# A differential-attention norm: its small VectorE operations moved behind the query's evacuation and cut from fifteen to eleven

## The chip, the cores and the metric

One core of a Trainium2 chip runs the whole kernel as one launch. The metric is device time in microseconds (us), the median of repeated runs. The engines are TensorE (PE for matmuls, PEld for weight loads), VectorE (DVE), ScalarE (ACT), GpSimd (POOL) and SyncE (SP), which issues most DMAs. Each engine works through its own queue strictly in order, so an instruction that waits holds back everything queued behind it on that engine.

## The reference, cut to what matters

Two layers run one after the other on 512 tokens of width 1024: sparse attention, then differential attention. Only the second is touched here:

```python
# differential attention: 8 heads, two softmax maps each, 128 value columns per head
p = softmax(where(dist >= 0, q @ k.T / 8 + bias, NEG))      # [heads, 2 maps, 512, 512]
a = p[:, 0] - lam * p[:, 1]
o = a @ v                                                   # per head: [512, 128]
o = rmsnorm(o, subln) * (1 - lambda_init)                   # over the 128 columns of a head
o = o.reshape(512, 1024) * silu(z)
return o @ w_out                                            # then x + rmsnorm(...)
# rmsnorm(o) = o / sqrt(mean(o * o) + 1e-6) * g
```

The kernel leaves the softmax undivided and divides later. With den0 and den1 the sums of the two maps' exponentials, it forms `p1 * lam * den0 / den1 - p0`, which is den0 times the wanted difference, up to the sign.

## The kernel before, in words

The differential layer goes through eight heads, and in a head through four blocks of 128 queries (units) in the order 3, 0, 2, 1. A unit covers 512, 128, 384 and 256 keys respectively. For each of its two maps, a unit has two score matmuls into an S bank of PSUM (lines 806 and 807; two S banks alternate between the maps), one DVE instruction that adds the bias and takes the row minimum (line 798), and one ACT exponential with its sum (line 800). After the second map DVE takes the reciprocal (1147), a factor (1148) and the difference (1149, in SBUF). TensorE then transposes the difference (1157), ACT copies it out (1159), and TensorE multiplies it with the values (1167). ACT copies a head's result o out of PSUM (1171).

Between these, a runner inserts the input projections of later heads: one job (`mjob`) is 24 matmuls of 512 columns (line 197). When a job is over, POOL splits the next raw weights into a high and a low part (lines 164 and 166, four pieces each), and the job's PSUM result is evacuated. For a query job that is `evac_q`: for each of two map halves ACT writes the rounded part (line 99) and then DVE the remainder (line 428), both by turns on the same bank. A unit's first score matmul (line 806) of the next head needs this remainder.

The norm is done once for a pair of heads. `dhead1` has eight ACT squares with sums (1179), then the small DVE operations on tiles of 128 by 8: two products with the reciprocal of den0 (1183), the mean and epsilon (320), an inverse square root from an integer start value by two correction steps (322 to 334), and a last product (1186). Then come eight products of o with the factor and the gate (1190, 128x128 each, both operands in SBUF). `dhead2` transposes o on TensorE (1198) and splits it again on ACT and DVE (99, 1201) as an operand of the output projection.

`dhead1` of heads 0 and 1 is issued in head 2 after the second unit, that of heads 2 and 3 in head 4, that of 4 and 5 in head 6, and that of 6 and 7 after the last head. The program is written in this order with priorities, and a scheduler sets the order of each engine's queue when the kernel is built. `issue_after(ins)` keeps the instructions of a block behind `ins` on its engine.

Of the kernel before, what the change touches and what calls it, by code (L numbers as in the profile page):

```python
# [57 lines left out]
EPS = 1e-6  # L58
# [9 lines left out]
def trunk(ctx: ExitStack, tc: tile.TileContext, x, table, npre, npost, w_in, pe_k, w1_k, w2_k,  # L68
# [248 lines left out]
    def rsqrt(y, ss, n, scale):  # L317

        m = small(n, tag="rs1")
        nc.vector.tensor_scalar(m, ss, scale, EPS, op0=OP.mult, op1=OP.add)  # L320
# [4 lines left out]
        w = small(n, tag="rs4")  # L325
        nc.vector.tensor_tensor(q, y, y, op=OP.mult)
        nc.vector.tensor_tensor(q, q, m, op=OP.mult)
        nc.vector.tensor_scalar(q, q, -0.5, 1.5, op0=OP.mult, op1=OP.add)
        nc.vector.tensor_tensor(y, y, q, op=OP.mult)
        nc.vector.tensor_tensor(q, y, y, op=OP.mult)  # L330
        nc.vector.tensor_tensor(q, q, m, op=OP.mult)
        nc.vector.tensor_scalar(w, q, 0.375, -1.25, op0=OP.mult, op1=OP.add)
        nc.vector.tensor_tensor(w, w, q, op=OP.mult)
        nc.vector.scalar_tensor_tensor(y, w, 1.875, y, op0=OP.add, op1=OP.mult)
# [87 lines left out]
    def evac_q(get, h0):  # L422
        def f(p):
            for j in range(2):
                t = get(h0 + j)
                a = slice(64 * j, 64 * j + 64)
                hi(t[0:64], p[a], 0.125)
                nc.vector.scalar_tensor_tensor(t[64:128], p[a], 0.125, t[0:64].bitcast(F32),
                                               op0=OP.mult, op1=OP.subtract)
# [283 lines left out]
    def turn_small():  # L713
# [7 lines left out]
        nc.scalar.activation(subT, pp[:, 0:8], AF.Copy, scale=-0.5 * (1.0 - LAMBDA_INIT))  # L721
# [402 lines left out]
    class DUnit:  # L1124
# [8 lines left out]
        def a(self, m):  # L1133
# [7 lines left out]
            self.P.append(softmap(s, n, 2 * h + m, qb, st[:, m:m + 1], st[:, 4 + m:5 + m]))  # L1141
            if m:
                p0, p1 = self.P
                if h % 2 == 0 and self.first:
                    T["rr", h // 2] = small(16, tag="drr", bufs=2)
                rr = T["rr", h // 2].rearrange("p (m c) -> p c m", m=2)[:, h % 2 * 4 + qb]
                nc.vector.reciprocal(rr, st[:, 4:6])
                nc.vector.tensor_scalar(st[:, 8:9], rr[:, 1:2], lam, st[:, 4:5], op0=OP.mult, op1=OP.mult)
# [25 lines left out]
    def dhead1(h0):  # L1174
# [6 lines left out]
        rr = T["rr", h0 // 2][:, 0:8]  # L1181
        for _ in range(2):
            nc.vector.tensor_tensor(ss, ss, rr, op=OP.mult)
        r = small(8, tag="drs")
        rsqrt(r, ss, 8, 1.0 / 128)
        nc.vector.tensor_tensor(r, r, rr, op=OP.mult)
# [93 lines left out]
```

## Time and profile before

| | |
|---|---|
| time, median of 3 runs | 656.49 us (655.78 to 656.52) |
| profiled execution, its own time | 655.29 us |
| span of its trace | 653.3 us |
| mean granted TensorE clock | 0.995 of full speed |
| TensorE busy | 635.7 us, 97% of the span |
| VectorE, ScalarE, GpSimd busy | 406.2, 344.7 and 401.4 us |

The differential heads run from about 424 to 601 us of the span, and the output projection fills the rest. A row of a timeline gives the start and duration of an instruction, its engine and line, what it writes and reads, and in brackets the idle time before it with what ended it.

### The profile page before, as it was taken

To read this page: it belongs to the slowest core of one execution; us is meant where nothing else is said; L and a number is where in the kernel's file an instruction comes from. 1 tells how busy PE (TensorE), PEld (TensorE's weight loads), DVE (VectorE), ACT (ScalarE), POOL (GpSimd) and SP (SyncE) were. 2 spreads that over 40 slices of the span, in tenths; PEclk is the share of its full clock that TensorE was granted. 3 is DMA by queue.
4 is the path that set the end of the run, shared out by engine and by line. 5 is a ranking of instruction groups with operands and counts; after the bars stand their busy time and mean duration, and the time that the engine had idled before them with its cause. 6 is when DMAs were issued, how large, how long until landed. Compare 5 with 4: busy or idle time off the path is not lost.

```text
span 653.3 us, 11250 instructions
## 1 busy us (share of the span) xinstructions
PE 635.7 (97%) x3767; PEld 554.5 (85%) x3767; DVE 406.2 (62%) x1190; ACT 344.7 (53%) x914; POOL 401.4 (61%) x675
## 2 busy tenths in 40 slices
PE   8999999999999999999999999999999998989996
PEld 6988888888888788788888899898987987879885
DVE  5512335678878878869788700235568669797634
ACT  6321234677667667768565411335474575668431
POOL 5458668778677687768585658848664554522300
PEclk9999999999999999999999999999999999989998
DMA  7636433213022121201962132423233232215302
GB/s 250 175 88 159 129 81 89 57 34 72 26 65 67 33 64 30 53 17 37 290 198 98 65 97 68 127 65 114 65 82 81 73 79 61 66 64 199 125 28 101
DMA packets 68847, 60.00 MB, mean 92 GB/s; under 512 B 3613, under 2 KB 60853, under 8 KB 68790
## 3 DMA queue, kind: packets, MB, share of 16 engines
q1 hardware_dynamic: 68068, 56.93, 29.7%
q10 hardware_dynamic: 722, 2.36, 0.9%
q8 instruction: 30, 0.49, 0.3%
q14 instruction: 27, 0.22, 0.1%
HBM read 54.52 MB, written 4.76 MB: 91 GB/s over the span
## 4 chain that ended last, share of the span: by engine, by line
PE 85%; DVE 8%; ACT 3%; issue 2%; DMA 1%; SPq 0%; DVEq 0%; ACTq 0%
PE mm L197 31%; PE mm L220 12%; PE mm L474 6%; PE S L220 6%; PE av L876 6%; PE T L862 5%; PE S L807 4%; PE S L806 4%; PE S L474 3%; PE av L1167 2%; PE T L727 1%; PE T L1157 1%; DMA wraw<-in_nsa_w_in_dram 1%; DVE stk L104 1%; DVE P L798 1%
## 5 line engine op out<-in xcount | busy, mean ns | idle before, releaser
L166 POOL TENSOR_TENSOR wlo<-wraw,whi 128x256 fp32r<-128x256 f32 (+2 forms) x247 | 182.7, 767 | 23.7 <-ACT whi L162 23.1
L164 POOL TENSOR_SCALAR whi<-wraw 128x256 fp32r<-128x256 f32 (+1 forms) x240 | 96.5, 428 | 101.4 <-PE mm L197 58.5
L800 ACT ACTIVATE P<-P,st 128x512 f32<-128x512 f32 (+3 forms) x192 | 107.4, 560 | 83.9 <-DVE st L798 83.1
L856 POOL TENSOR_SCALAR P<-P,st,gate 128x512 f32<-128x512 f32 (+3 forms) x128 | 80.2, 638 | 25.7 <-DVE st L853 17.6
L798 DVE CUSTOM_DVE_ANT_0 P<-S,BT 128x128 f32<-128x128 f32 (+2 forms) x144 | 59.7, 418 | 28.5 <-PE S L807 26.2
L197 PE MATMUL mm<-bigA,whi 128*128 128x512 f32 x192 | 77.1, 402 | 0.1
L197 PE MATMUL mm<-bigA,wlo 128*128 128x512 f32 x192 | 75.5, 393 | 0.0
L197 PE MATMUL mm<-bigB,whi 128*128 128x512 f32 x192 | 75.3, 392 | 0.0
L104 DVE TENSOR_TENSOR PT<-T,PT 128x512 fp32r<-128x512 f32 x84 | 56.9, 685 | 7.3 <-ACT PT L99 5.0
L876 PE MATMUL av<-PT,bigE 128*128 128x512 f32 x160 | 57.3, 418 | 0.1
L104 DVE TENSOR_TENSOR stk<-mm,stk 64x512 fp32r<-64x512 f32 x32 | 22.0, 689 | 52.2 <-ACT stk L99 51.8
L99 ACT ACTIVATE PT<-T 128x512 fp32r<-128x512 f32 x84 | 48.3, 593 | 8.8 <-PE T L862 6.1
L862 PE MATMUL T<-ident,P 128*128 128x128 f32 x320 | 52.1, 272 | 0.0
L197 PE MATMUL mm<-bigF,whi 128*128 128x512 f32 x128 | 51.4, 402 | 0.0
L99 ACT ACTIVATE stk<-mm 64x512 fp32r<-64x512 f32 x64 | 37.9, 592 | 25.1 <-PE mm L197 13.9
L862 PEld LDWEIGHTS T<-ident,P 128*128 128x128 f32 x320 | 40.8, 140 | 11.8 <-DVE PT L104 0.2
L220 PE MATMUL mm<-whi,bigF 128*128 128x256 f32 x176 | 50.7, 289 | 0.1
L197 PE MATMUL mm<-bigE,whi 128*128 128x512 f32 x128 | 50.4, 394 | 0.0
L220 PE MATMUL mm<-wlo,bigF 128*128 128x256 f32 x176 | 50.3, 286 | 0.0
L197 PE MATMUL mm<-bigF,wlo 128*128 128x512 f32 x128 | 50.2, 392 | 0.0
L220 PE MATMUL mm<-whi,bigE 128*128 128x256 f32 x176 | 49.8, 284 | 0.0
L197 PEld LDWEIGHTS mm<-bigB,whi 128*128 128x128 f32 x192 | 36.1, 188 | 8.0
(295 smaller groups left out, 1646.4 us busy)
## 6 DMA issues: line engine op xcount, KB each, us to landing
wraw<-in_diff_w_in_dram SPq DMA_DIRECT2D x31, 512.0 KB, 3.9
wraw<-in_nsa_w_in_dram SPq DMA_DIRECT2D x26, 512.0 KB, 3.8
BT<-rd SPq DMA_DIRECT2D x32, 128.0 KB, 3.2
wraw<-in_diff_w_out_dram SPq DMA_DIRECT2D x5, 512.0 KB, 3.8
wraw<-in_nsa_w_out_dram SPq DMA_DIRECT2D x4, 512.0 KB, 3.5
bigD<-in_x_dram SPq DMA_DIRECT2D x4, 512.0 KB, 3.8
x1d<-bigD ACTq DMA_DIRECT2D x4, 512.0 KB, 2.6
bigF<-x1d SPq DMA_DIRECT2D x4, 512.0 KB, 6.2
```

The lines of the kernel that those rows point to most:

```text
L99: return nc.scalar.activation(dst, src, AF.Copy, scale=scale)
L104: nc.vector.tensor_tensor(dst, src, h.bitcast(F32), op=OP.subtract)
L164: nc.gpsimd.tensor_scalar(h[:, a:b], v, 1.0, 0.0, op0=OP.mult, op1=OP.add)
L166: e.tensor_tensor(l[:, a:b], v, h[:, a:b].bitcast(F32), op=OP.subtract)
L197: T["mm"] = nc.tensor.matmul(p[:, a:b], wt[:, k, :], u[:, k, a:b], start=(k == 0 and j == 0), stop=(k == KD - 1 and j == 2)).ins
L220: nc.tensor.matmul(acc[t], u[:, k0 + k, t * 128:(t + 1) * 128], wt[:, k, :], start=(ci == 0 and k == 0 and j == 0 and t % per == 0), stop= ...
L474: nc.tensor.matmul(p, U[u][:, k, t * 128:(t + 1) * 128], wt[wi], start=start and j == 0, stop=stop and j == 2, skip_group_check=True)
L798: nc.vector.tensor_tensor_reduce(out=o, in0=i0, in1=b, op0=OP.add, op1=OP.min, scale=-1.0, scalar=BIG, accum_out=nm)
L800: nc.scalar.activation(pt[:, :n], pt[:, :n], AF.Exp, bias=nm, scale=-1.0, accum_out=den)
L856: NORM(nc, i, br, qb).tensor_scalar(self.P[i][:, :n], self.P[i][:, :n], st[:, 8 + i:9 + i], gate[:, NT - 1 - qb, c:c + 1], op0=OP.mult, op ...
L862: T["tmark"] = nc.tensor.transpose(p[:, j * 128:(j + 1) * 128], self.P[j][:, kb * 128:(kb + 1) * 128], ident).ins
L876: nc.tensor.matmul(av, T["V"][:, br, kb, g, :], p, start=(br == 0 and kb == 0 and j == 0), stop=(br == 1 and kb == qb and j == 1))
```

## The change

The norm's formula is multiplied through by den0. In place of o/den0 · 1/sqrt(mean(o²)/den0² + eps) the kernel computes o · 1/sqrt(mean(o²) + eps·den0²): two operations form `den0 * den0 * eps + ss / 128`, and the products with the reciprocal go. The correction steps are written with fewer instructions; a constant factor 0.375 of the second one is moved into `subT`. The fifteen small DVE operations of a norm become eleven, nine of which have two tensors in SBUF as operands. The sum den0 is written by the exponential straight into a tile that lives for a pair of heads, and the reciprocal in a unit takes one column in place of two.

`dhead1` keeps only the eight ACT squares and stays where it was. The rest is now `dnorm`, called after a head's last projection job, under `issue_after(T["qe"])`, where `T["qe"]` is the last remainder of a query evacuation (line 428 before, 426 now). `dhead2` for the same heads moves from the third and fourth units of heads 2, 4 and 6 to the second and third units of heads 3, 5 and 7.

```diff
-    def rsqrt(y, ss, n, scale):
+    def rsqrt(y, ss, d, n, scale):
         m = small(n, tag="rs1")
-        nc.vector.tensor_scalar(m, ss, scale, EPS, op0=OP.mult, op1=OP.add)
+        nc.vector.scalar_tensor_tensor(m, d, EPS, d, op0=OP.mult, op1=OP.mult)
+        nc.vector.scalar_tensor_tensor(m, ss, scale, m, op0=OP.mult, op1=OP.add)
         sh = small(n, I32, tag="rs2")
...
-        nc.vector.tensor_tensor(q, y, y, op=OP.mult)
-        nc.vector.tensor_tensor(q, q, m, op=OP.mult)
-        nc.vector.tensor_scalar(q, q, -0.5, 1.5, op0=OP.mult, op1=OP.add)
-        nc.vector.tensor_tensor(y, y, q, op=OP.mult)
-        nc.vector.tensor_tensor(q, y, y, op=OP.mult)
-        nc.vector.tensor_tensor(q, q, m, op=OP.mult)
-        nc.vector.tensor_scalar(w, q, 0.375, -1.25, op0=OP.mult, op1=OP.add)
-        nc.vector.tensor_tensor(w, w, q, op=OP.mult)
-        nc.vector.scalar_tensor_tensor(y, w, 1.875, y, op0=OP.add, op1=OP.mult)
+        nc.vector.tensor_tensor(q, y, m, op=OP.mult)
+        nc.vector.scalar_tensor_tensor(q, q, -0.5, y, op0=OP.mult, op1=OP.mult)
+        nc.vector.scalar_tensor_tensor(y, q, 1.5, y, op0=OP.add, op1=OP.mult)
+        nc.vector.tensor_tensor(q, y, m, op=OP.mult)
+        nc.vector.tensor_tensor(q, q, y, op=OP.mult)
+        nc.vector.scalar_tensor_tensor(q, q, -10.0 / 3, q, op0=OP.add, op1=OP.mult)
+        nc.vector.scalar_tensor_tensor(y, q, 5.0, y, op0=OP.add, op1=OP.mult)
@@ class DUnit, a(m)
-                nc.vector.reciprocal(rr, st[:, 4:6])
-                nc.vector.tensor_scalar(st[:, 8:9], rr[:, 1:2], lam, st[:, 4:5], op0=OP.mult, op1=OP.mult)
+                nc.vector.reciprocal(st[:, 6:7], st[:, 5:6])
+                nc.vector.tensor_scalar(st[:, 8:9], st[:, 6:7], lam, den, op0=OP.mult, op1=OP.mult)
@@ def dhead1(h0), after the eight squares
-        rr = T["rr", h0 // 2][:, 0:8]
-        for _ in range(2):
-            nc.vector.tensor_tensor(ss, ss, rr, op=OP.mult)
+        T["dss"] = ss
+
+    def dnorm(h0):
+        ss = T["dss"]
         r = small(8, tag="drs")
-        rsqrt(r, ss, 8, 1.0 / 128)
-        nc.vector.tensor_tensor(r, r, rr, op=OP.mult)
+        rsqrt(r, ss, T["den", h0 // 2], 8, 1.0 / 128)
         for i in range(8):
...
-            if i in (2, 3) and h in (2, 4, 6):
+            if i in (1, 2) and h in (3, 5, 7):
                 dhead2(h - 4 + i)
             carry = u
         run.upto(dends[h])
+        if h in (2, 4, 6):
+            with tc.issue_after(T["qe"]):
+                dnorm(h - 2)
     carry.t(0)
     carry.v(0)
     dhead1(6)
+    dnorm(6)
     dhead2(6)
```

Line numbers of the rows after the norm's own are two lower in the changed file (798 is 796, 1190 is 1188). Up to the second unit of head 2 every engine's queue holds the same work in the same order, and POOL and SP do so throughout.

First place, DVE's queue at the end of head 2. Names: `rs`, `drs` and `dss` are the norm's small tiles, `drr` the sums or reciprocals, `stk` a query or key operand, `PT` a head's o, `P` the softmax tiles, `st` a unit's columns. Before:

```order
L332 TENSOR_SCALAR rs_5936<-rs_5935 128x8
L798 ISA P,st<-S,BT_80 128x256
L798 ISA st 128x1
L333 TENSOR_TENSOR rs_5936<-rs_5936,rs_5935 128x8
L428 SCALAR_TENSOR_TENSOR stk<-mm,stk 64x512
L334 SCALAR_TENSOR_TENSOR drs<-rs_5936,drs 128x8
L1147 RECIPROCAL drr<-st 128x2
L1186 TENSOR_TENSOR drs<-drs,drr 128x8
L1148 TENSOR_SCALAR st<-drr,lam,st 128x1
L1190 SCALAR_TENSOR_TENSOR PT<-PT,drs,bigB 128x128 x8
L1149 SCALAR_TENSOR_TENSOR P<-P,st 128x256
L428 SCALAR_TENSOR_TENSOR stk<-mm,stk 64x512
```

The same place on DVE in the changed kernel:

```order
L796 ISA P,st<-S,BT_80 128x256
L796 ISA st 128x1
L426 SCALAR_TENSOR_TENSOR stk<-mm,stk 64x512
L1145 RECIPROCAL st<-st 128x1
L1146 TENSOR_SCALAR st<-st,lam,drr 128x1
L1147 SCALAR_TENSOR_TENSOR P<-P,st 128x256
L426 SCALAR_TENSOR_TENSOR stk<-mm,stk 64x512
L320 SCALAR_TENSOR_TENSOR rs_6023<-drr 128x8
L321 SCALAR_TENSOR_TENSOR rs_6023<-dss,rs_6023 128x8
L323 TENSOR_SCALAR rs_6026<-rs_6023 128x8
L324 TENSOR_SCALAR drs<-rs_6026 128x8
L796 ISA P,st<-S,BT_80 128x512
```

All of the norm has moved behind both remainders; the other seven small operations and the eight products follow the last row shown, ahead of the second 128x512 row of line 796.

Second place, DVE's queue at the start of head 5, from the remainder on. Before, where the norm of heads 2 and 3 is already over:

```order
L428 SCALAR_TENSOR_TENSOR stk<-mm,stk 64x512
L798 ISA P,st<-S,BT_79 128x512
L798 ISA st 128x1
L1201 SCALAR_TENSOR_TENSOR bigD<-T,subT,bigC 128x512 x2
L798 ISA P,st<-S,BT_79 128x512
L798 ISA st 128x1
L798 ISA P,st<-S,BT_79 128x128
```

And now, from the seventh of the eleven operations on:

```order
L329 TENSOR_TENSOR drs<-drs,rs_6581 128x8
L796 ISA P,st<-S,BT_79 128x512
L796 ISA st 128x1
L330 TENSOR_TENSOR rs_6587<-rs_6587,drs 128x8
L331 SCALAR_TENSOR_TENSOR rs_6587<-rs_6587 128x8
L332 SCALAR_TENSOR_TENSOR drs<-rs_6587,drs 128x8
L1188 SCALAR_TENSOR_TENSOR PT<-PT,drs,bigB 128x128 x8
L1145 RECIPROCAL st<-st 128x1
L796 ISA P,st<-S,BT_79 128x128
```

The eight products now stand ahead of the 128x128 bias rows that free the S banks of the second unit.

## Rows read from the trace of the kernel before

**Rows 1.** Page, busy us (share of the span) x instructions of each engine
```profile
PE 635.7 (97%) x3767; PEld 554.5 (85%) x3767; DVE 406.2 (62%) x1190; ACT 344.7 (53%) x914; POOL 401.4 (61%) x675
```

**Rows 2.** Waits of PE, 410 to 605 us: total us, times, longest us
```profile
PE S L806 <- DVE stk L428: 4.7, 4, 1.9
```

**Rows 3.** Windows: us, busy of PE PEld DVE ACT POOL, PEclk, DMA share, GB/s
```profile
540.00:550.00 10.00, 8.07 (x46) 6.43 (x46) 9.74 (x32) 4.90 (x11) 4.27 (x8) 1.00 0.23 69
...
580.00:590.00 10.00, 8.29 (x54) 7.91 (x55) 8.21 (x32) 4.47 (x13) 0.00 (x1) 0.83 0.16 52
```

**Rows 4.** Timeline of PE, ends of heads 4 and 6: start, duration, instruction
```profile
544.44 0.50 PE L806 MATMUL S<-stk 128*128 128x512 f32 x1 [1.93 <-DVE stk L428]
...
581.71 0.79 PE L806 MATMUL S<-stk 128*128 128x512 f32 x1 [1.90 <-DVE stk L428]
...
582.73 0.41 PE L220 MATMUL mm<-whi,bigF 128*128 128x256 f32 x1
582.94 0.41 PE L220 MATMUL mm<-wlo,bigF 128*128 128x256 f32 x1
...
584.86 0.40 PE L220 MATMUL mm<-whi,bigF 128*128 128x256 f32 x1
...
585.82 0.28 PE L220 MATMUL mm<-wlo,bigF 128*128 128x256 f32 x1
585.94 0.28 PE L220 MATMUL mm<-whi,bigE 128*128 128x256 f32 x1
```

**Rows 5.** Timeline of DVE, end of head 2
```profile
494.79 0.69 DVE L332 TENSOR_SCALAR rs<-rs 128x8 f32<-128x8 f32 x1
...
496.20 0.69 DVE L428 SCALAR_TENSOR_TENSOR stk<-mm,stk 64x512 fp32r<-64x512 f32 x1
496.92 0.62 DVE L334 SCALAR_TENSOR_TENSOR drs<-rs,drs 128x8 f32<-128x8 f32 x1
...
497.85 2.18 DVE L1190 SCALAR_TENSOR_TENSOR PT<-PT,drs,bigB 128x128 f32<-128x128 f32 x8
...
500.46 0.69 DVE L428 SCALAR_TENSOR_TENSOR stk<-mm,stk 64x512 fp32r<-64x512 f32 x1
```

**Rows 6.** Timeline of POOL, end of head 2
```profile
493.21 1.52 POOL L164 TENSOR_SCALAR whi<-wraw 128x256 fp32r<-128x256 f32 x4 [3.62 <-PE mm L197]
494.70 2.83 POOL L166 TENSOR_TENSOR wlo<-wraw,whi 128x256 fp32r<-128x256 f32 x4
```

**Rows 7.** Timeline of DVE, end of head 6
```profile
578.74 1.28 DVE L329 TENSOR_TENSOR drs<-drs,rs 128x8 f32<-128x8 f32 x1
...
580.97 0.69 DVE L428 SCALAR_TENSOR_TENSOR stk<-mm,stk 64x512 fp32r<-64x512 f32 x1
```

**Rows 8.** Timeline of ACT, end of head 6
```profile
576.80 0.28 ACT L1159 ACTIVATE PT<-T 128x128 f32<-128x128 f32 x1
...
578.01 1.15 ACT L162 ACTIVATE whi<-wraw 128x512 fp32r<-128x512 f32 x2 [0.44 <-issue]
579.06 0.57 ACT L99 ACTIVATE stk<-mm 64x512 fp32r<-64x512 f32 x1
```

**Rows 9.** Timeline of DVE, norm of heads 6 and 7
```profile
611.55 0.17 DVE L332 TENSOR_SCALAR rs<-rs 128x8 f32<-128x8 f32 x1
611.75 0.17 DVE L333 TENSOR_TENSOR rs<-rs,rs 128x8 f32<-128x8 f32 x1
...
612.36 3.23 DVE L1190 SCALAR_TENSOR_TENSOR PT<-PT,drs,bigB 128x128 f32<-128x128 f32 x8
```

**Rows 10.** Timeline of POOL, the same stretch
```profile
613.91 1.53 POOL L166 TENSOR_TENSOR wlo<-wraw,whi 128x512 fp32r<-128x512 f32 x1 [3.23 <-ACT whi L162]
```

**Rows 11.** Timeline of PE, two projection matmuls in head 2
```profile
495.50 0.39 PE L197 MATMUL mm<-bigF,whi 128*128 128x512 f32 x1
495.73 0.39 PE L197 MATMUL mm<-bigF,wlo 128*128 128x512 f32 x1
```

**Rows 12.** Groups by form, whole span: count, busy us, mean ns, idle before
```profile
L798 DVE CUSTOM_DVE_ANT_1 P<-S,BT 128x512 f32<-128x512 f32 x48 | 33.0, 688 | 14.6 <-PE S L807 12.8 <-POOL wlo L166 0.8 <-POOL whi L164 0.2
```

More of the change, by code (lines that the diff above doesn't have):

```diff
@@ L324, in rsqrt @@
         q = small(n, tag="rs3")
-        w = small(n, tag="rs4")
-        nc.vector.tensor_tensor(q, y, y, op=OP.mult)
-        nc.vector.tensor_tensor(q, q, m, op=OP.mult)
-        nc.vector.tensor_scalar(q, q, -0.5, 1.5, op0=OP.mult, op1=OP.add)
-        nc.vector.tensor_tensor(y, y, q, op=OP.mult)
-        nc.vector.tensor_tensor(q, y, y, op=OP.mult)
-        nc.vector.tensor_tensor(q, q, m, op=OP.mult)
-        nc.vector.tensor_scalar(w, q, 0.375, -1.25, op0=OP.mult, op1=OP.add)
-        nc.vector.tensor_tensor(w, w, q, op=OP.mult)
-        nc.vector.scalar_tensor_tensor(y, w, 1.875, y, op0=OP.add, op1=OP.mult)
+        nc.vector.tensor_tensor(q, y, m, op=OP.mult)
[5 more added lines that the diff above has]
+        nc.vector.scalar_tensor_tensor(y, q, 5.0, y, op0=OP.add, op1=OP.mult)
     epst = const.tile([128, 1], F32, name="epst")
@@ L427, in f @@
                 hi(t[0:64], p[a], 0.125)
-                nc.vector.scalar_tensor_tensor(t[64:128], p[a], 0.125, t[0:64].bitcast(F32),
-                                               op0=OP.mult, op1=OP.subtract)
+                T["qe"] = nc.vector.scalar_tensor_tensor(t[64:128], p[a], 0.125, t[0:64].bitcast(F32),
+                                                         op0=OP.mult, op1=OP.subtract).ins
         return f
@@ L720, in turn_small @@
         nc.tensor.transpose(pp[:, 0:8], sub8, ident[0:8, 0:8])
-        nc.scalar.activation(subT, pp[:, 0:8], AF.Copy, scale=-0.5 * (1.0 - LAMBDA_INIT))
+        nc.scalar.activation(subT, pp[:, 0:8], AF.Copy, scale=-0.5 * 0.375 * (1.0 - LAMBDA_INIT))
     def compress(i, key):
@@ L1140, in a @@
             s = scores(T["dq", 2 * h + m], kh, kl, qb, n)
-            self.P.append(softmap(s, n, 2 * h + m, qb, st[:, m:m + 1], st[:, 4 + m:5 + m]))
+            if h % 2 == 0 and self.first and m == 0:
+                T["den", h // 2] = small(8, tag="drr", bufs=2)
+            den = T["den", h // 2][:, h % 2 * 4 + qb:h % 2 * 4 + qb + 1]
+            self.P.append(softmap(s, n, 2 * h + m, qb, st[:, m:m + 1], st[:, 5:6] if m else den))
             if m:
                 p0, p1 = self.P
-                if h % 2 == 0 and self.first:
-                    T["rr", h // 2] = small(16, tag="drr", bufs=2)
-                rr = T["rr", h // 2].rearrange("p (m c) -> p c m", m=2)[:, h % 2 * 4 + qb]
-                nc.vector.reciprocal(rr, st[:, 4:6])
-                nc.vector.tensor_scalar(st[:, 8:9], rr[:, 1:2], lam, st[:, 4:5], op0=OP.mult, op1=OP.mult)
+                nc.vector.reciprocal(st[:, 6:7], st[:, 5:6])
+                nc.vector.tensor_scalar(st[:, 8:9], st[:, 6:7], lam, den, op0=OP.mult, op1=OP.mult)
                 nc.vector.scalar_tensor_tensor(p0[:, :n], p1[:, :n], st[:, 8:9], p0[:, :n],
```

## The prediction

> **What bounds the kernel now.** I read the page's busy times first. TensorE is busy for 97% of the span [rows 1], so work taken off another engine is worth only what it takes out of TensorE's waits or gives back of its clock. The changed instructions run between 484 and 618 us. I therefore asked next for TensorE's waits between 410 and 605 us: one line answers, four waits of 4.7 us in total, all of a first score matmul (806) for the DVE remainder of a query evacuation (428) [rows 2]. Two of the four are 1.93 us at the end of head 4 and 1.90 us at the end of head 6 [rows 4]; the rest, 0.86 us, stands at the end of head 2. These are the three heads in which a norm stands in DVE's queue. The ends of heads 1, 3 and 5, with the same evacuation and no norm, show no such wait.
>
> The windows show a second loss [rows 3]. Between 540 and 550 us the granted clock stays at 1.00 through the 1.93 us wait. Between 580 and 590 us it is 0.83: behind the 1.90 us wait, 256-column matmuls start 0.21 us apart against 0.12 us a little later [rows 4]. TensorE is at the lower of its two levels, 1.2 GHz, from 581.7 to about 585.1 us, and about half of these 3.4 us is lost, less what stood at full speed at the edges: 1.5 us. So what this change can win is 4.7 + 1.5 = 6.2 us.
>
> DVE's timeline shows why the remainder is late. At the end of head 2, small operations on 128x8 take 0.69 us (332) and 0.62 us (334) [rows 5] while GpSimd splits weights [rows 6]; the same kinds take 0.17 us and follow each other every 0.20 us when it does not [rows 9]. Between the two remainders, the eight products hold DVE for another 2.18 us [rows 5]. At the end of head 6 a single small operation takes 1.28 us [rows 7].
>
> **The change part by part.** *Fewer small operations.* Four are gone per norm, 4 x 0.20 = 0.8 us of DVE time [rows 9], and 3.2 us over four norms. By itself this is worth nothing to TensorE except inside the four waits, where I count it with the move.
>
> *The move, first remainder.* At the ends of heads 2 and 4 nothing of the norm is left ahead of it. The remainder then follows the exponential and the rounded half on ACT, as in the odd heads, and I take all of 0.86 and 1.93 us as won. At the end of head 6 something else is late next. ACT first splits a piece of the output weights, two operations of 1.15 us together, then writes the rounded half in 0.57 us [rows 8], and DVE takes 0.69 us [rows 7]. The splitting starts at 578.01 us; a copy of 0.28 us is now in ACT's queue ahead of the rounded half [rows 8]. That is 1.15 + 0.28 + 0.57 + 0.69 = 2.7 us, so the remainder ends at 580.7 or a little later, against 581.66 us before (580.97 + 0.69). TensorE wants it at 579.8 us (581.71 - 1.90), so 0.9 us of waiting is left. The second remainder there stands behind a 128x512 bias row, about 0.69 us [rows 12], which itself waits for the first score. TensorE has only six 256-column matmuls and five small ones to fill this, so I add 0.25 us. Together 1.15 of 1.90 us stays, with 0.5 and 1.9 us as bounds.
>
> *The clock.* With 1.9 us of waiting in one piece turned into 0.9 us I take the clock as staying up: 1.5 us won. The trace bounds this from both sides: a 1.93 us wait left the clock alone and a 1.90 us wait did not, so the loss can also stay.
>
> *What the norm does in its new place.* It stands at the opening of heads 3, 5 and 7 between the bias rows (798) that free the S banks. In head 5, from the start of the second 512-column score to the 384-column score that needs a bank freed behind the products, TensorE has 18 projection matmuls of 0.23 us [rows 11], 4.1 us, two score matmuls of the same length, 0.5 us, and six short ones of at most 0.12 us [rows 4], 0.7 us: 5.3 us. On DVE stand 0.5 us until the score is there, 0.69 us for its bias row [rows 12], three small operations of 0.20 us [rows 9] and the products' 2.18 us [rows 5]; a reciprocal and the 128-column bias row I set at 0.5 us together, under the 0.69 us of the long one. That makes 4.5 us, and 0.8 us to spare if DVE is on time. But between the remainders stands the unit's difference and behind them the first of the eleven operations. Both have two operands in SBUF and fall into the burst in which GpSimd splits weights behind each projection job, 1.52 + 2.83 = 4.35 us in pieces of 0.38 and 0.71 us [rows 6]. Each can wait for a piece; from that I put DVE 0.4 to 1.1 us late. The products then start 2.2 to 2.9 us after that second score, and the next burst starts some 3.5 us after it (twelve matmuls of 0.23 us and the scores). Of eight products at 0.27 us, three to six are left, and each waits for a piece. Three cost about 0.3 us of TensorE's time beyond what is to spare, six about 2.6 us; I take 1.0 us. In head 3 the S banks have more room, the unit's transpose comes first, and I take 0.5 us between 0 and 1.5. In head 7 the products ran between the two 512-column bias rows already before, without a wait of TensorE, so nothing is added to the 1.15 us.
>
> That operations with both operands in SBUF wait for GpSimd is shown by the last norm too: eight products take 3.23 us instead of 2.18 us where one GpSimd operation of 1.53 us falls among them [rows 9, 10]. The Trainium skill has a rule for this ("SBUF — State Buffer", section "Who interferes with whom"): a VectorE instruction with two SBUF inputs contends with a GpSimd instruction that reads SBUF, and the one that comes second waits for the other's end. By that rule nine of the eleven operations and all eight products can be blocked wherever they stand, and the trace agrees; a reading by durations alone, at 0.17 us each, would leave the 1.5 us of heads 3 and 5 out of the sum.
>
> *The end.* The last eight transposes of o now stand around the 71st matmul of the output projection's first half in place of the 62nd, and the 73rd already needs their result. Bounds are 0 and 0.4 us, since a copy and a remainder of about 0.7 us each must fit into some 1.3 us of matmuls and transposes; I take 0.2 us. *The rest* (a reciprocal of one column, the exponential's sum in another tile, the constant in `subT`) costs nothing: same count, engine and place.
>
> Sum: 6.2 won, less 1.15 + 1.0 + 0.5 + 0.2 = 2.85, is 3.35 us. The profiled execution took 655.29 us (span 653.3 and 2.0 around it), so it would come to 651.9; it was 1.2 us under the median of 656.49, and from the median I predict 653.1 us.
>
> **Rivals.** *The gain is eaten up* (655.2 to 657.8 us). In heads 3 and 5 the new waits come to 2.4 us together, as the products meet the burst, and the clock still falls at the end of head 6: 6.2 - 1.5 - 1.15 - 0.2 - 2.4 = 0.9 us, so 655.6 us. For it speaks that every piece of the burst is longer than a small operation; against it, that the first products start ahead of the burst.
>
> *Slower.* The products of heads 3 and 5 run wholly inside GpSimd's burst. The mechanism is the shared wait at one place, the S bank of the second unit. It costs 2.6 us in head 5 and 1.5 us in head 3, and a wait of that length takes the clock down once more for 1.5 us, while the old loss at head 6 stays but for 0.75 us: 4.7 - 1.15 - 2.6 - 1.5 - 0.2 - 1.5 = -2.25, so 658.7 us. It decides from about six of eight products behind the burst's start on. The section of the Trainium skill named above would give this case. Against it speaks the order: 0.8 us to spare in head 5.
>
> *The waits go and nothing comes back*: 6.2 - 0.65 = 5.5 us, 651.0 us. For it speaks that the openings of heads 3 and 5 held two 512-column remainders (1201) at this place before, about 0.7 us each by the bias row of that size [rows 12], without a wait. That work has moved to later units.
>
> **How the numbers follow.** What three runs of this kernel can tell from no change is about 0.2%, 1.3 us, so faster means below 655.2. Forecast with waits partly back: 0.45; nothing back: 0.16; eaten up: 0.25; slower: 0.14. Of the third, 0.02 lies below the bound and 0.23 within it, so faster 0.63, same 0.23, slower 0.14. The forecast's own range is 651.3 to 655.0. With the others, less a tenth at either end, it is 650.7 to 657.2 us.
>
> **What would show it.** Right: no wait of the first score for the remainder at the ends of heads 2 and 4, one below 1.2 us at the end of head 6, and a granted clock of 1.00 there. New waits of score matmuls for bias rows (798, now 796), or of transposes for the difference, in heads 3 and 5, with the products lengthened beyond 2.18 us, give their price directly. The forecast is wrong if these sum to over 3 us, if the clock falls at a new place, or if the first score still waits where the norm has gone.

## The result, and the profile after

The changed kernel took 650.6 and 651.63 us (median 651.1) beside 656.49 us before: ratio 0.9926 (95% 0.9898 to 0.9954). Run twice more, each time beside the kernel before, it took 651.21 us (ratio 0.9921, 0.9908 to 0.9934) and 651.77 us (0.9943, 0.9926 to 0.9960). So it is faster by 3.7 to 5.4 us, under 1%; the forecast was 653.1, and the time lies inside the range of 650.7 to 657.2. Two disturbed executions of 1590.38 and 888.31 us are left out (in the first, the only one of the two with a trace, the projection matmuls took 0.83 us in place of 0.39), and the rows of the changed kernel below are of a later execution (span 649.4 us).

Page of the changed kernel, busy us (share) x instructions, answering [rows 1]:

```profile
PE 635.1 (98%) x3767; PEld 552.7 (85%) x3767; DVE 403.9 (62%) x1174; ACT 344.6 (53%) x914; POOL 400.5 (62%) x675
```

The shares say little (TensorE has 98% where it had 97%); the waits of PE between 405 and 605 us do (total us, times, longest), answering [rows 2]:

```profile
PE S L804 <- DVE stk L426: 0.5, 1, 0.5
PE mm L220 <- DVE stk L104: 0.3, 1, 0.3
PE T L1155 <- DVE P L1147: 0.2, 1, 0.2
PE av L1165 <- ACT PT L1157: 0.2, 1, 0.2
```

The one line of 4.7 us has become four lines of 1.2 us. Windows of the changed kernel, answering [rows 3], with the same columns; the first one runs from the first score matmul of the layer to the end of its last output projection matmul:

```profile
426.58:643.12 216.54, 215.31 (x1302) 189.86 (x1300) 143.59 (x408) 118.38 (x334) 96.43 (x160) 1.00 0.28 88
...
580.00:590.00 10.00, 9.97 (x82) 9.62 (x81) 9.31 (x39) 6.83 (x18) 1.28 (x1) 1.00 0.09 34
540.00:550.00 10.00, 10.00 (x58) 8.59 (x57) 8.74 (x32) 5.49 (x14) 4.98 (x9) 1.00 0.25 77
```

The same stretch of the kernel before:

```profile
425.81:646.98 221.17, 216.48 (x1302) 191.71 (x1300) 145.75 (x424) 118.35 (x334) 96.38 (x160) 0.99 0.27 86
```

With the same 1302 matmuls the stretch is 4.63 us shorter: idle time fell from 221.17 - 216.48 = 4.69 to 1.23 us, and the matmuls' own busy time by 1.17 us. The granted clock of 580 to 590 us is 1.00 where it was 0.83.

Timeline of PE in the changed kernel, answering [rows 4] (start, duration, instruction, idle before it): the waits that are left in head 3 and at the end of head 6, and 256-column matmuls behind the latter, 0.12 us apart, where they stood 0.21 us apart before [rows 4].

```profile
508.75 0.66 PE L1155 MATMUL T<-ident,P 128*128 128x128 f32 x4 [0.21 <-DVE P L1147]
...
510.48 0.36 PE L220 MATMUL mm<-whi,bigF 128*128 128x256 f32 x1 [0.29 <-DVE stk L104]
...
578.52 0.50 PE L804 MATMUL S<-stk 128*128 128x512 f32 x1 [0.49 <-DVE stk L426]
...
582.04 0.28 PE L220 MATMUL mm<-whi,bigE 128*128 128x256 f32 x1
582.16 0.28 PE L220 MATMUL mm<-whi,bigF 128*128 128x256 f32 x1
```

Timeline of DVE, answering [rows 5] and [rows 7]: both remainders of head 2 with the products behind them, the products of head 5, and the end of head 6.

```profile
494.95 0.68 DVE L426 SCALAR_TENSOR_TENSOR stk<-mm,stk 64x512 fp32r<-64x512 f32 x1
...
497.31 0.69 DVE L426 SCALAR_TENSOR_TENSOR stk<-mm,stk 64x512 fp32r<-64x512 f32 x1
...
501.27 4.23 DVE L1188 SCALAR_TENSOR_TENSOR PT<-PT,drs,bigB 128x128 f32<-128x128 f32 x8
505.42 0.68 DVE L796 CUSTOM_DVE_ANT_1 P<-S,BT 128x512 f32<-128x512 f32 x1
...
548.17 2.47 DVE L1188 SCALAR_TENSOR_TENSOR PT<-PT,drs,bigB 128x128 f32<-128x128 f32 x8
...
550.63 0.27 DVE L796 CUSTOM_DVE_ANT_0 P<-S,BT 128x128 f32<-128x128 f32 x1
...
576.44 1.31 DVE L166 TENSOR_TENSOR wlo<-wraw,whi 128x512 fp32r<-128x512 f32 x1
577.78 0.68 DVE L426 SCALAR_TENSOR_TENSOR stk<-mm,stk 64x512 fp32r<-64x512 f32 x1
```

Timelines of POOL and of ACT at the same places, answering [rows 6] and [rows 8]:

```profile
501.51 1.62 POOL L164 TENSOR_SCALAR whi<-wraw 128x256 fp32r<-128x256 f32 x4 [2.94 <-PE mm L197]
503.10 3.00 POOL L166 TENSOR_TENSOR wlo<-wraw,whi 128x256 fp32r<-128x256 f32 x4
...
549.49 1.78 POOL L164 TENSOR_SCALAR whi<-wraw 128x256 fp32r<-128x256 f32 x4 [3.85 <-PE mm L197]
...
575.90 1.30 POOL L166 TENSOR_TENSOR wlo<-wraw,whi 128x512 fp32r<-128x512 f32 x1 [4.30 <-ACT whi L162]
```

```profile
575.21 1.14 ACT L162 ACTIVATE whi<-wraw 128x512 fp32r<-128x512 f32 x2
576.25 0.25 ACT L1157 ACTIVATE PT<-T 128x128 f32<-128x128 f32 x1
576.41 0.58 ACT L99 ACTIVATE stk<-mm 64x512 fp32r<-64x512 f32 x1
```

Three things stand here. In head 3 all but the first of the products fall into GpSimd's burst: 4.23 us in place of 2.18, from 501.27 on, with the burst from 501.51 to 506.1. In head 5 they start 1.3 us ahead of the burst and take 2.47 us. At the end of head 6 the rounded half is ready at 576.99 us, but VectorE is in its own split of a weight piece (166), which takes 1.31 us in place of 0.69 while GpSimd works on its half at the same time (575.90 to 577.20), and so the remainder starts at 577.78. The same split in the kernel before, behind GpSimd's half:

```profile
580.17 0.69 DVE L166 TENSOR_TENSOR wlo<-wraw,whi 128x512 fp32r<-128x512 f32 x1
```

### The profile page after: what moved, and what is told of

It is laid out like the page before. It is cut to its first block, busy times and chain, and to the rows that moved or that the text cites. A ratio compares the mean times of both kernels' runs of the same rounds, so it can differ in the third digit from the quotient of the medians.

```text
span 1588.4 us, 11231 instructions
## 1 busy us (share of the span) xinstructions
PE 1580.8 (100%) x3767; PEld 1157.4 (73%) x3767; DVE 401.9 (25%) x1174; ACT 356.0 (22%) x914; POOL 393.2 (25%) x675
## 4 chain that ended last, share of the span: by engine, by line
PE 99%; DVE 0%; issue 0%; DVEq 0%; ACT 0%
PE mm L197 36%; PE mm L220 12%; PE mm L472 7%; PE S L472 6%; PE av L874 6%; PE S L220 6%; PE T L860 6%; PE S L805 5%; PE S L804 5%; PE av L1165 3%; PE T L725 1%; PE T L1155 1%; PE T L388 1%; PE T L1196 1%; PE T L220 0%; PE mm L315 0%
## 5 line engine op out<-in xcount | busy, mean ns | idle before, releaser
L197 PE MATMUL mm<-bigA,whi 128*128 128x512 f32 x192 | 158.6, 828 | 0.0
L197 PE MATMUL mm<-bigA,wlo 128*128 128x512 f32 x192 | 158.6, 826 | 0.0
L197 PE MATMUL mm<-bigB,whi 128*128 128x512 f32 x192 | 157.9, 822 | 0.0
L874 PE MATMUL av<-PT,bigE 128*128 128x512 f32 x160 | 127.9, 884 | 0.0
L860 PE MATMUL T<-ident,P 128*128 128x128 f32 x320 | 119.5, 535 | 0.0
L197 PE MATMUL mm<-bigF,whi 128*128 128x512 f32 x128 | 109.4, 854 | 0.0
L197 PEld LDWEIGHTS mm<-bigA,wlo 128*128 128x128 f32 x192 | 70.7, 368 | 31.8 <-issue 28.7
L197 PEld LDWEIGHTS mm<-bigA,whi 128*128 128x128 f32 x192 | 68.7, 358 | 27.4 <-issue 25.4
L220 PEld LDWEIGHTS mm<-wlo,bigF 128*128 128x128 f32 x176 | 75.2, 427 | 2.2 <-issue 1.9
L220 PEld LDWEIGHTS mm<-whi,bigF 128*128 128x128 f32 x176 | 75.2, 428 | 2.2 <-issue 1.7
```

What stands on the lines that cost most here:

```text
L197: T["mm"] = nc.tensor.matmul(p[:, a:b], wt[:, k, :], u[:, k, a:b], start=(k == 0 and j == 0), stop=(k == KD - 1 and j == 2)).ins
L220: nc.tensor.matmul(acc[t], u[:, k0 + k, t * 128:(t + 1) * 128], wt[:, k, :], start=(ci == 0 and k == 0 and j == 0 and t % per == 0), stop= ...
L860: T["tmark"] = nc.tensor.transpose(p[:, j * 128:(j + 1) * 128], self.P[j][:, kb * 128:(kb + 1) * 128], ident).ins
L874: nc.tensor.matmul(av, T["V"][:, br, kb, g, :], p, start=(br == 0 and kb == 0 and j == 0), stop=(br == 1 and kb == qb and j == 1))
```

## The experiments

The theory to test: the place of the norm against the remainder carries the gain, and it is cheap as long as the eight products run ahead of GpSimd's next burst. Its rivals: the smaller number of operations carries the gain; or the new place costs as much as forecast and something else was won. In the table the stretch runs from the second remainder of head 0 (before the first changed instruction) to the start of the first of the last two VectorE instructions, in one profile. Two profiles of the changed kernel give it as 220.78 and 220.75 us, while what lies ahead of it, alike in all these kernels, differed by up to 3 us from profile to profile; so the stretch tells smaller differences than the whole time, though each of the other kernels has one profile alone. TensorE's idle time is that of a window like the one above. The ratio compares the executions and need not be the quotient of two medians.

| kernel | median us | ratio to before (95%) | stretch us | PE idle us |
|---|---|---|---|---|
| before | 655.4 to 656.5 | 1 | 225.41 | 4.69 |
| after_again | 651.21 | 0.9921 (0.9908 to 0.9934) | 220.78 | 1.23 |
| after_ref | 651.77 | 0.9943 (0.9926 to 0.9960) | 220.75 | 1.19 |
| ops_only | 658.28 | 1.0035 (1.0022 to 1.0048) | 230.01 | 5.31 |
| move_only | 654.79 | 0.9984 (0.9971 to 0.9996) | 225.23 | 4.33 |
| no_edge | 657.16 | 1.0021 (1.0009 to 1.0034) | 226.78 | 5.49 |
| pad4 | 653.99 | 0.9973 (0.9959 to 0.9987) | 224.12 | 3.44 |
| prod_moved | 651.23 | 0.9943 (0.9920 to 0.9966) | 221.49 | 2.14 |
| prod_moved_old | 651.72 | 0.9954 (0.9936 to 0.9972) | 222.09 | 2.22 |
| no_norm | 650.07 | 0.9921 (0.9898 to 0.9945) | 219.44 | 0.78 |
| split_pool | 650.39 | 0.9922 (0.9896 to 0.9947) | 220.10 | 1.15 |
| best | 650.36 | 0.9921 (0.9903 to 0.9938) | 221.06 | 1.58 |
| best2 | 650.23 | 0.9914 (0.9892 to 0.9937) | 218.72 | 0.22 |

**The changed kernel again** (after_again, after_ref; no edit).

> The changed kernel once more, for an undisturbed profile. Theory A (the forecast's sum with fewer new waits): at the ends of heads 2 and 4 no wait of the first score for the remainder (before 0.86 and 1.93 us), under 1.2 us at the end of head 6 (before 1.90), granted clock 1.00 in the window 580 to 590 us (before 0.83), and new waits of score matmuls for bias rows (796) of under 0.7 us in heads 3 and 5 together; ratio to the kernel before 0.991 to 0.994. Rival B (the waits come back as the forecast said and something else is won): new waits of 1.0 us in head 5 and 0.5 us in head 3, and a gain of 1 to 2 us at a place the forecast does not name.

> The changed kernel beside the two that follow, on the same chip, so that differences under 1 us can be told. Both theories: about 651 us, ratio to the kernel before 0.991 to 0.994.

Theory A: no wait at the ends of heads 2 and 4, 0.49 us at the end of head 6, clock 1.00, 0.5 us in head 3 and nothing in head 5. Two details differ: the 0.5 us are not waits for bias rows, and the second ratio, 0.9943, lies a hair above the range.

**The new operations at the old place** (ops_only).

```diff
-            if i in (1, 2) and h in (3, 5, 7):
+            if i in (2, 3) and h in (2, 4, 6):
                 dhead2(h - 4 + i)
-        if h in (2, 4, 6):
-            with tc.issue_after(T["qe"]):
-                dnorm(h - 2)
```

(and the body of `dnorm` is back in `dhead1`)

> The eleven-operation formula at the old place: the norm is issued whole behind the second unit of heads 2, 4 and 6, and the transposes of o stay in the third and fourth units. Theory A (the move carries the gain): in DVE's queue of heads 2 and 4 the whole norm with its eight products (2.18 us) now stands ahead of the first remainder, where before the products stood behind it; four operations less give back 0.8 us at 0.20 us each, or 2.8 us at 0.69 us each beside GpSimd. So the first score's wait at the ends of heads 2 and 4 is as long as before or longer by up to 1.4 us each, and the ratio to the kernel before is 0.999 to 1.003. Rival B (the smaller number of operations carries it): the four waits fall from 4.7 to under 2 us, ratio 0.993 to 0.996.

It is slower than before, 1.0022 to 1.0048, at the upper end of theory A's range or beyond, and rival B is out. But the waits are not those that theory A names. The first score waits less than before in each head (0.73 us in head 2, 0.95 in head 4, 1.39 + 0.39 in head 6, 3.5 us in all against 4.7), and 1.8 us of new waits are of the transposes of o (line 1192 here) for the products. Timelines of DVE and PE in this kernel at the end of head 2:

```profile
490.85 0.66 DVE L323 TENSOR_SCALAR rs<-rs 128x8 int32<-128x8 int32 x1
...
496.30 4.20 DVE L1184 SCALAR_TENSOR_TENSOR PT<-PT,drs,bigB 128x128 f32<-128x128 f32 x8
...
500.87 0.68 DVE L426 SCALAR_TENSOR_TENSOR stk<-mm,stk 64x512 fp32r<-64x512 f32 x1
```

```profile
499.03 0.33 PE L1192 MATMUL T<-ident,PT 128*128 128x128 f32 x1 [0.16 <-DVE PT L1184]
499.76 1.12 PE L1192 MATMUL T<-ident,PT 128*128 128x128 f32 x4 [0.40 <-DVE PT L1184]
501.61 0.50 PE L804 MATMUL S<-stk 128*128 128x512 f32 x1 [0.73 <-DVE stk L426]
```

and its windows (columns as in [rows 3]):

```profile
500.00:510.00 10.00, 9.27 (x38) 7.30 (x38) 6.56 (x17) 5.94 (x13) 1.88 (x5) 0.83 0.28 66
550.00:560.00 10.00, 9.05 (x40) 7.32 (x41) 7.50 (x22) 4.70 (x12) 0.51 (x2) 0.84 0.18 54
```

With the new formula the scheduler put all eight products ahead of the first remainder, and there they fall into the burst that starts at 495.11 us. A chain that is shorter by itself became the longer one on the path. The idle time is 5.31 us in place of 4.69, and no single wait is longer than 1.39 us (before 1.93), but waits lie close together twice, as in the rows above and in head 4 (three of 0.40 us within 2 us), and the clock falls both times (0.83 and 0.84).

The transposes of o stand at their old place here and in the kernel before, and at the new one in all other kernels of the table. No run moves them alone, so what their move by itself is worth is not shown.

**The old operations at the new place** (move_only).

```diff
+        for _ in range(2):
+            nc.vector.tensor_tensor(ss, ss, rr, op=OP.mult)
         r = small(8, tag="drs")
-        rsqrt(r, ss, T["den", h0 // 2], 8, 1.0 / 128)
+        rsqrt(r, ss, 8, 1.0 / 128)
+        nc.vector.tensor_tensor(r, r, rr, op=OP.mult)
```

(in `dnorm`, with the old `rsqrt`, sums and constant in `subT`)

> The old fifteen-operation formula with the two products by the reciprocal, moved as in the change: behind the last remainder of a query evacuation, and the transposes into heads 3, 5 and 7. Theory A (the move carries the gain, and the new place has room): the four waits go as in the changed kernel, four more small operations at 0.20 us put the products 0.8 us later, and what that costs stays under 1 us over heads 3, 5 and 7; ratio to the kernel before 0.991 to 0.995. Rival B (the new place is tight, and the shorter formula is what makes the products fit ahead of GpSimd's burst): new waits of 1.5 to 4 us for bias rows behind the products in heads 3 and 5, ratio 0.996 to 1.003.

Rival B: 0.9984, waits of 1.6 us for bias rows and 4.33 us of idle time in all. The clock no longer falls, but the stretch is only 0.18 us shorter than before. Timelines of DVE and PE in head 5 (GpSimd's burst starts at 549.29 us):

```profile
550.11 4.36 DVE L1194 SCALAR_TENSOR_TENSOR PT<-PT,drs,bigB 128x128 f32<-128x128 f32 x8
554.39 0.28 DVE L798 CUSTOM_DVE_ANT_0 P<-S,BT 128x128 f32<-128x128 f32 x1
```

```profile
554.73 0.44 PE L806 MATMUL S<-stk 128*128 128x384 f32 x1 [0.89 <-DVE st L798]
```

The products start 0.8 us behind the burst's start in place of 1.3 us ahead of it, and take 4.36 us.

**Without the edge** (no_edge).

```diff
-            with tc.issue_after(T["qe"]):
-                dnorm(h - 2)
+            dnorm(h - 2)
```

> The changed kernel without issue_after: the norm is called at the same place of the program, but the scheduler may put it ahead of the remainders. In DVE's queue of heads 4 and 6 it then stands around them: ten of eleven operations ahead of or between the remainders, in head 4 also four of the eight products (1.1 us) ahead of the second one; in head 2 it stays behind. Theory A (the order against the remainders is what counts): waits of the first score come back at the ends of heads 4 and 6, 0.5 to 1.9 us each, ratio to the kernel before 0.994 to 0.998. Rival B (the later call alone is enough, since the operations start late): waits under 0.3 us in sum, ratio 0.990 to 0.993.

The expectation misread the order at the end of head 2: there too the norm moved ahead of the remainders, with all eight products ahead of the first (3.93 us for seven, a bias row, then the eighth). Timeline of PE:

```profile
500.66 0.50 PE L804 MATMUL S<-stk 128*128 128x512 f32 x1 [3.06 <-DVE stk L426]
```

That single wait is longer than any before, and the clock falls behind it (0.83 between 500 and 510 us). Slower by 1.0009 to 1.0034, which is beyond theory A's own 0.994 to 0.998: calling the norm later without the edge loses the whole gain.

**Four more small operations** (pad4).

```diff
         rsqrt(r, ss, T["den", h0 // 2], 8, 1.0 / 128)
+        if h0 < 6:
+            for _ in range(2):
+                nc.vector.tensor_tensor(r, r, ones8, op=OP.mult)
+                nc.vector.tensor_tensor(r, r, ones8, op=OP.mult)
```

> The changed kernel with four more small operations of 128x8 (products with a tile of ones) between the eleven operations and the eight products of the norms in heads 3, 5 and 7: fifteen operations as before, but with the new formula. Theory A (in head 5 the eleven operations just fit ahead of GpSimd's burst): the products start about 0.8 us later there (four times 0.20), fall into the burst, take 3.5 to 4.4 us in place of 2.47, and a score matmul of the second or third unit waits 0.5 to 1.0 us for its bank; in head 3, where the products fall into the burst already, and at the end of head 6 at most 1 us more; time 1.5 to 3.5 us above the changed kernel's, ratio to the kernel before 0.994 to 0.998. Rival B (the moved old formula was slow for another reason, its two products with the reciprocal or its two-column reciprocal): under 0.8 us above the changed kernel's, ratio 0.992 to 0.993.

Theory A by its times: 653.99 us, stretch 3.3 us longer. Timelines of DVE and PE in head 5:

```profile
548.84 0.75 DVE L1149 SCALAR_TENSOR_TENSOR P<-P,st 128x512 f32<-128x512 f32 x1
...
549.90 4.50 DVE L1194 SCALAR_TENSOR_TENSOR PT<-PT,drs,bigB 128x128 f32<-128x128 f32 x8
```

```profile
554.66 0.45 PE L806 MATMUL S<-stk 128*128 128x384 f32 x1 [0.75 <-DVE st L798]
```

So the number of operations, whatever the formula, accounts for 3.3 of the 4.45 us by which move_only's stretch is longer; the other 1.1 us stay open. Fifteen put the products behind the burst's start, eleven don't, but not by their 0.8 us alone: counted from the second 512-column bias row the products start 1.9 us later than in the changed kernel (3.15 against 1.22 us). Besides the four operations the scheduler put a bias row, the reciprocal, the factor and the difference (line 1149, 0.75 us) ahead of them, as it did in move_only. Whether 0.8 us alone would have brought them into the burst is not shown. The price is spread: 0.75 us in head 5, 0.62 us at the end of head 6, and 0.3 to 0.45 us each at two places in head 3, one in head 7 and two of the output projection, where the changed kernel had less or nothing.

**Only the products moved** (prod_moved with the new formula, prod_moved_old with the old one).

```diff
+        r = small(8, tag="drs")
+        rsqrt(r, ss, T["den", h0 // 2], 8, 1.0 / 128)
-        T["dss"] = ss
+        T["dss"] = r

     def dnorm(h0):
-        ss = T["dss"]
-        r = small(8, tag="drs")
-        rsqrt(r, ss, T["den", h0 // 2], 8, 1.0 / 128)
+        r = T["dss"]
```

> The new formula with its eleven small operations at the old place, and only the eight products (and the transposes of o) moved behind the last remainder. Theory A (in the old place it is the products inside GpSimd's burst that hold the remainder): the waits of the first score at the ends of heads 2 and 4 fall under 0.5 us each, the one at the end of head 6 stays at 1 to 1.5 us, and the products run ahead of the burst in heads 3 and 5; ratio to the kernel before 0.992 to 0.996. Rival B (the small operations, each of which can wait for a GpSimd piece, hold the remainder as much): waits of 0.6 us or more at the ends of heads 2 and 4, ratio 0.997 or above.

> The old formula, its fifteen small operations at the old place, and only the eight products (and the transposes of o) moved behind the last remainder. With the runs before it this separates the two parts: the products' place, and the number of small operations. Theory A (the products' place carries most of the gain, and four operations more at the old place cost what they cost before, a wait of 0.6 us at the end of head 2, as much or less at the end of head 4, and 1.9 us at the end of head 6, with the clock there): ratio to the kernel before 0.994 to 0.997. Rival B (the small operations at the old place lay beside other work in the old formula too, except at the end of head 6): ratio 0.992 to 0.994. Rival C (with fifteen the remainder is as late as before): 0.998 to 1.001.

With the new formula theory A: with eleven operations at the old place no first score waits at the ends of heads 2 and 4. With the old one the ratio lies in theory A's range, but the waits lie between A and rival B: 0.25 and 0.37 us at the ends of heads 2 and 4, 1.05 us at the end of head 6 in place of 1.9, and the clock does not fall. Timeline of DVE and waits of PE (480 to 600 us) in prod_moved_old:

```profile
497.92 2.19 DVE L1194 SCALAR_TENSOR_TENSOR PT<-PT,drs,bigB 128x128 f32<-128x128 f32 x8
```

```profile
PE S L806 <- DVE stk L428: 1.7, 3, 1.0
```

The products run their plain 2.19 us ahead of the burst in heads 3 and 5. What stays is the end of head 6, 1.05 us with the old formula and 0.92 + 0.18 with the new one, where the whole norm behind the remainder is better (0.49 + 0.03); with the new one 0.39 us in head 5 and 0.65 us in the output projection come up besides. In the stretch, moving the products alone gives 3.32 us (old formula) or 3.92 us (new), the change 4.65 us.

**No norm in the new place** (no_norm).

```diff
-        if h in (2, 4, 6):
-            with tc.issue_after(T["qe"]):
-                dnorm(h - 2)
```

> The changed kernel without the eleven operations and eight products of the norms of heads 0 to 5; the squares, the transposes and everything else stay, so heads 0 to 5 go into the output projection unnormalised and ungated. It bounds from below what the norm costs in its new place. Theory A (the new place costs 0.5 us in head 3 and nothing in head 5 and 7): 0.3 to 0.8 us under the changed kernel, ratio to the kernel before 0.990 to 0.992. Rival B (VectorE's 9 us of norm cost more than the waits in heads 3 and 5 show, by later evacuations or releases): 1.5 us or more under the changed kernel, ratio below 0.990.

By the waits theory A, by the stretch neither. No wait is left in heads 3 and 5, but the first score at the end of head 6 now waits longer, behind the same split of a weight piece (PE):

```profile
578.07 0.50 PE L804 MATMUL S<-stk 128*128 128x512 f32 x1 [0.76 <-DVE stk L426]
```

The stretch is 1.34 us shorter, between theory A's 0.8 and rival B's 1.5: 0.45 us of it idle time, the rest in the matmuls' busy time (214.41 against 215.31 us). So by this one profile the norm costs about 1.3 us at most in its new place, though 14.8 us of VectorE's busy time are gone from the window (128.77 against 143.59 us). The ratios of the two kernels don't differ.

**The weight piece at the end of head 6 to GpSimd** (split_pool).

```diff
-                e = nc.vector if i in self.quick and (i + a) % 2 else nc.gpsimd
+                e = nc.vector if i in self.quick and i not in self.whole and (i + a) % 2 else nc.gpsimd
...
+            ws.whole.add(j.first - 4)
```

> The changed kernel with the low part of one piece of the output weights, at the end of head 6, taken from VectorE to GpSimd, so that no weight operation stands ahead of the remainder on VectorE. Theory A (the 0.49 us left of the first score's wait at the end of head 6 is VectorE's own split of 1.31 us, which stands directly ahead of the remainder and is itself held by GpSimd): the remainder starts at the end of the rounded half on ScalarE, 0.8 us earlier, the wait is gone, and the time is 0.3 to 0.6 us lower than the changed kernel's; ratio to the kernel before 0.991 to 0.992. Rival B (ScalarE's split and rounded half set that end, as the forecast had it): the wait stays within 0.2 us of 0.49, same time.

Theory A for the wait. Timeline of DVE and waits of PE (480 to 600 us):

```profile
577.21 0.68 DVE L427 SCALAR_TENSOR_TENSOR stk<-mm,stk 64x512 fp32r<-64x512 f32 x1 [0.50 <-ACT stk L99]
```

```profile
PE av L1168 <- ACT PT L1160: 0.6, 1, 0.6
PE mm L221 <- DVE stk L104: 0.3, 1, 0.3
PE T L1158 <- DVE P L1150: 0.2, 1, 0.2
```

VectorE is now waiting for the rounded half, and the first score for nobody. But 0.6 us came up in head 7, from ScalarE, which there waits for the output weights (its timeline):

```profile
594.71 0.63 ACT L163 ACTIVATE wx<-P 128x512 fp32r<-128x512 f32 x1 [1.04 <-DMA P<-in_diff_w_out_dram]
```

With that the idle time is nearly what it was (1.15 against 1.23 us). The stretch is 0.68 us shorter, most of it in the matmuls' busy time (214.72 against 215.31 us), for which no row gives a cause; the ratio of 0.9922 can't be told from the changed kernel's.

**Put together** (best: small operations at the old place in heads 2 and 4; best2, shown here: in head 2 alone; both with the weight piece on GpSimd).

```diff
+        if h0 < 2:
+            drs()
...
     def dnorm(h0):
+        if not h0 < 2:
+            drs()
+        r = T["drs"]
```

> A kernel put together from the earlier runs: in heads 2 and 4 the eleven small operations at the old place and only the eight products behind the remainder, so that the products run ahead of GpSimd's burst in heads 3 and 5; in head 6 the norm behind the remainder as in the change, and the low part of the weight piece there on GpSimd. Theory A (the waits left in the changed kernel, 0.5 us in head 3 and 0.49 us at the end of head 6, go and nothing takes their place): 0.5 to 1.2 us under the changed kernel of this call, ratio to the kernel before 0.989 to 0.992. Rival B (other waits of the same size come up behind them, as 0.39 us in head 5 and 0.6 us in head 7 did in the runs that moved only one of the two): within 0.4 us of the changed kernel.

> As the kernel before it in the record, but only head 2 keeps the eleven small operations at the old place (products behind the remainder, ahead of the burst); heads 4 and 6 are as in the change, and the low part of the weight piece at the end of head 6 is on GpSimd. Theory A: the 0.5 us of head 3 and the 0.49 us at the end of head 6 are gone, no wait comes up in head 5, and in head 7 a product with the values waits 0.6 to 1.1 us for ScalarE, which itself waits for the output weights' DMA; the stretch from the second remainder of head 0 to the last VectorE row takes 219.6 to 220.4 us (changed kernel 220.78 and 220.75, before 225.41), ratio to the kernel before 0.990 to 0.993. Rival B: what head 3 gives back is lost again in head 7, since the DMA lands at the same moment: 220.4 to 220.9 us.

In best, rival B by the stretch: 0.39 us in head 5 and 1.09 us in head 7 (ScalarE behind the same DMA) took the place of what went, although its median is 1.4 us under that of the changed kernel beside it (650.36 against 651.77). In the two profiles its stretch is 0.3 us longer, and what lies ahead of it, where the two kernels are alike, 0.9 us shorter. Medians and profiles disagree here, and which holds stays open. In best2 theory A for heads 3, 5 and 6, and its wait of 0.6 to 1.1 us in head 7 did not come: waits of PE, 424 to 645 us, are one line:

```profile
PE av L1168 <- ACT PT L1160: 0.2, 1, 0.2
```

Its stretch of 218.72 us is below theory A's range and 2.06 us under the changed kernel's, 1.0 us of it idle time and the rest in the matmuls' busy time (214.26 against 215.31 us). With 650.23 us and 0.9914 (0.9892 to 0.9937) it is the fastest by median of the kernels that keep the norm, but the interval doesn't part it from the changed kernel; only the one profile does.

## Why the prediction was nearly right, and what in it was not

*What could be won* was right in place and nearly in size. The four waits are gone but for 0.49 + 0.03 us at the end of head 6 (the 0.03 are the idle time of 580 to 590 us), and the clock stays at 1.00 there. The clock's 1.5 us can't be read off one pair of traces: the matmuls' busy time fell by 1.17 us, but between kernels whose clock never falls here it differs by 2.4 us (214.26 in best2, 216.67 in move_only), for reasons that stay open. The 66 executions of the kernel before, timed in four sets beside the later runs, speak for the forecast's size: 49 have a mean granted clock of 0.992 to 0.996 and a median of 656.14 us, 17 one of 0.997 or more and 654.42 us. Read so, the clock falls in most executions, not in all, and costs about 1.7 us (0.8 to 2.3 in each of the four sets). The changed kernel's are all at 0.997 to 0.999.

*The step that failed is the 2.85 us that should come back; 1.23 us did.* By time alone the rival "the waits go and nothing comes back", with 651.0 us and a chance of 0.16, stands nearer to the measured 651.1, 651.21 and 651.77 us than the forecast's 653.1; by the waits the truth lies between its 0.65 us and the forecast's 2.85.

- Head 5, 1.0 us forecast, nothing measured. The order and the margin were read rightly, the delay was not. The second score starts at 545.73 us, the products 2.44 us behind it (forecast 2.2 to 2.9), the burst 3.76 us behind it (forecast 3.5). At 0.27 us from one to the next, six of the eight start ahead of the burst, one more than forecast for the early end. Read one by one, the sixth starts at 549.48, just ahead of GpSimd's first piece, which takes 0.60 us in place of 0.41. Only the last two alternate with pieces, short ones of the high part, and then follow each other every 0.40 us: 0.13 us more each, not a whole piece. So all eight took 2.47 us, and GpSimd's high parts 1.78 us in place of 1.52. The bias rows follow at 550.63, ahead of the 384-column score at 551.30. The forecast's prices, 0.3 us for three held products and 2.6 us for six, stand there without a working, and no run shows them.
- Head 6, 1.15 us forecast, 0.52 measured, and by another hand. ScalarE's split and rounded half were forecast to set the end; relative to the moment at which TensorE wants the remainder they came about 1 us earlier than before (578.03 - 575.21 = 2.82 us against 579.8 - 578.01 = 1.8 us); why is not shown. What was late next is VectorE's own split of the weight piece, which stood in the queue before too and was overlooked. Before, a small operation of the norm had waited for GpSimd there (1.28 us, [rows 7]) and the split then took 0.69; now the split waits in its place. split_pool shows it.
- Head 3, 0.5 us forecast, 0.50 measured (0.21 + 0.29), though the products fell into the burst, the case that the rival "slower" had priced at 1.5 us here. That the number fits is luck. The products grew by 2.05 us: four follow each other every 0.40 us beside high parts, three every 0.74 us beside low ones. The waits came at the transpose of the difference and behind an evacuation (104), not at an S bank; the projection matmuls covered the other 1.5 us.
- The end, 0.2 us forecast, 0.05 measured; another 0.16 us in head 7, not forecast, is ScalarE behind a DMA.

The sum by these: 4.69 - 1.23 = 3.46 us of waits and 1.17 us in the matmuls, 4.63 us, against 3.35 forecast; between medians timed side by side it is 4.8 and 3.7 us.

*Fewer operations.* The forecast gave the four operations less 0.8 us of VectorE time and no worth but inside the old waits. That was wrong in kind: at the old place the shorter formula makes the kernel slower (ops_only), at the new place it is worth 4.45 us of the stretch (move_only against the change), 3.3 of them by the number of operations (pad4), which decides with the scheduler's order whether the products meet the burst.

*The lock.* Products of 2.18 us take 3.2 to 3.3 us with one GpSimd operation of a 128x512 piece among them and 4.1 to 4.5 us inside a burst (2.47 us where only the last two meet it). The rule in the Trainium skill ("SBUF — State Buffer", section "Who interferes with whom") that a VectorE instruction with two SBUF inputs and a GpSimd instruction that reads SBUF exclude each other fits this. The section adds that the order of issue decides who blocks; the trace agrees instruction by instruction in head 5, where GpSimd's first piece waited for the sixth product and the last two products for pieces, 0.26 us for GpSimd and 0.29 for VectorE in all. It also names `tensor_scalar` among the operations that, under conditions on their operands, can take the shared ports, which agrees with 0.66 us for one of 128x8 in ops_only, 0.17 elsewhere.

## What to carry to other kernels

Ask of every chain of small VectorE work not how long it is but which GpSimd burst it will meet, and what is queued behind it there: in head 5 the same eight products cost TensorE nothing when they start 1.3 us ahead of the burst, and 0.75 or 0.89 us when they start 0.6 or 0.8 us behind its start. Fix such an order by an edge: without one the scheduler put the shorter chain where it does harm, in no_edge and in ops_only. And when a wait goes, read the whole queue in front of the waiting instruction for what is late next, the weight work that was always there included.

## What the hardware showed beyond that

Idle time of TensorE isn't the whole price of a wait: ops_only waits 5.31 us where before waits 4.69, but its clock falls twice, and the same 1302 matmuls are busy for 220.46 us in place of 216.48. A wait of 1.93 us at the end of head 4 left the clock alone [rows 3, 4], 3.06 us in no_edge and three waits of 0.16, 0.40 and 0.73 us within 3 us in ops_only did not. What decides it was not tried.
